# Position rows and the softmax division on ScalarE, and a planner with turns at the shared port

## The chip, the core and the metric

One core of one Trainium2 chip. The time is device microseconds of one launch. The engines are TensorE (PE: matmuls and transposes), VectorE (DVE), ScalarE (ACT), GpSimd (POOL), and SyncE (SP), which issues the DMAs here. Each engine works through its own list of instructions in order and waits on semaphores for the others.

## The reference

A decoder block over 512 tokens of width 1024, with four groups of four heads of 64:

```python
hn = rms_norm(x, norm_gain)
proj = hn @ w_in                       # 1024 x 3844, split into the groups' q, k, v and gates
o_fox  = softmax(q k^T / 8 + c_i - c_j, causal) @ v          # f: c = cumsum of log_sigmoid(forget)
o_moba = softmax(q k^T / 8 + rel_bias[bucket(i - j)], top-3 blocks and own block) @ v   # m
o_sb   = stick-breaking weights, exp(log_sigmoid(z) + suffix sums of log_sigmoid(-z)) @ v   # s
o_swa  = softmax(q k^T / 8 + rel_bias[...], window 128, with a sink) @ v                # w
y = concat(o_fox * silu(fg), o_moba * silu(mg), o_sb * silu(sg), o_swa * silu(wg))
return x + y @ w_out
```

q and k of f, m and w are RMS-normalised per head. With 512 tokens the m heads have two blocks of 256, so that they see every earlier token. All is float32.

## The kernel before

Every float32 product is made from three `float32r` matmuls: an operand is split into a hi part (rounded, `hi_copy`, on ACT) and a lo part (the rest, `lo_part`, on DVE, or on POOL), and `mm3` sums hi x hi, hi x lo and lo x hi into one PSUM bank. In names, `wh_`, `xh`, `pth_`, `yh_` are hi parts and `wl_`, `xl`, `ptl_`, `yl_` lo parts.

Weights arrive in chunks of 512 KB (`raw_`), numbered over all sets in the order sv, sqk, fvf, fqk, fg, sg, mqk, mv, mg, wg, wqkv, o. For the chunks in `POOL_LO` POOL makes the lo part in pieces of 260 columns, for the others DVE in one instruction.

The program runs the groups in the order s, f, m, w, with the projections of later groups laid between the heads' work to keep PE busy. A head has four score tiles, one for each distance or block of 128 keys, 512, 384, 256 and 128 wide for s, f and m and at most 256 for w. `softmax_head` (f, m, w): scores on PE, a fused add and minimum on DVE (`pm`, `nm`: the negated maximum), exp with row sum on ACT (`sm`), reciprocal on DVE, multiplication by it, then four rounds of transposes on PE (`pT_`), their hi and lo parts (`pth_`, `ptl_`) and the product with v (`o_f`, `o_s` and so on). `sb_head` (s): Abs, Exp, Ln on ACT (`l_`), a maximum, a scan and a difference on DVE (`pm_s`), exp on ACT, then the same transposes. The first digit of a number in these names is the head, the second the tile. `sqk` holds the scaled q and k of the s heads, `qs_` and `k00` to `k11` their hi and lo halves. `frow`, `fS` and `fxb` carry the forget sums into the f heads. `oc_`, `gate_`: a head pair's output and its gate.

`rel_rows` spreads the 32 bucket values of the relative bias over 512 distances (`relrow`, 8 rows), writes them to DRAM and spreads them from there to 128 partitions, from where `load_band` reads each head's band. `relrow` lies in the buffer that `fxb0`, and so `fS`, uses later.

The program order isn't the order in which the engines run. All instructions are collected, `_steps` finds their dependences, and `_plan` simulates the engines with a cost for each instruction: at each step the engine that can start first takes, of its instructions that can start within `PATIENCE` ns of the earliest, the one of lowest priority number. That number is the place in the program plus `TURN` of the kind of work. `MARGIN` is added to the latency of a result that another engine waits for. DVE instructions with two operands in SBUF, and all of POOL's, also wait for one modelled port. `order_engines` fixes the planned order on each engine.

Of the kernel before, what the change touches and what calls it, by code (L numbers as in the profile page):

```python
# [12 lines left out]
AF = mybir.ActivationFunctionType  # L13
ALU = mybir.AluOpType
# [24 lines left out]
REL_AT = "fg"  # L39
SQK_BANKS, R_BANK = ["sc", "tp", "tp", "pv"], "pj"  # L40

RATE, OUTU = 4.54, 0.55

POOL_LO = {1, 4, 6, 9, 10, 12, 15, 16, 17, 19, 21, 23, 24, 34, 36, 37, 38}
PIECE = 260
DVE_SQ = {(1, 1), (2, 1), (3, 0), (3, 1)}

OCUT, WARM, WARM_GAPS = 2, 3, 8


TURN = {"xn": 207, "gate": 18, "qk": -250, "v": -71, "s": 14, "pt": -313, "ot": 134, "gap":
        100000, "y": 10, "fb": 5, "w": 108, "pv": 16, "oc": 186, "nat": 0, "proj": 61, "x": -110}
PATIENCE = {"Pool": 10, "PE": 54}

MARGIN = {"PE": 100, "Activation": 41}


BOUNDS = list(range(17)) + [21, 27, 35, 46, 59, 77, 99, 128, 166, 216, 280, 363, 470]
# [18 lines left out]
def block_kernel(ctx, tc, x, xT, w_in, w_out, small, rel, out):  # L77
    nc = tc.nc
# [72 lines left out]
    if WARM:  # L151
# [3 lines left out]
        pt = pv("warm")  # L155
# [109 lines left out]
    for n in LOADS.split():  # L265
        k = int(n[1:] or 0)
# [264 lines left out]
    def softmax_head(g, h, Q, K, V, vcol, bias, nblk):  # L531
        pm = sb.tile([P, 1280], F32, tag="pm", name=f"pm_{g}{h}", bufs=2)
        off, blocks = 0, {}
        for i in range(NT):
            w = nblk(i)
            n = w * P
            blocks[i] = (off, w)
            s, s2 = scores(g, h, i, n, Q, K)
            seg = pm[:, off:off + n]
            b = bias(i, n)  # L540
            if s2 is not None:
                nc.vector.tensor_tensor(seg, s2, b, op=ALU.add)
                b = seg
            nm = cp.tile([P, 1], F32, tag="nm", name=f"nm_{g}{h}{i}", bufs=4)
            sm = cp.tile([P, 1], F32, tag="sm", name=f"sm_{g}{h}{i}", bufs=4)

            init = nsk[:, h:h + 1] if g == "w" else 3.0e38
            nc.vector.tensor_tensor_reduce(seg, s, b, scale=-1.0, scalar=init,  # L548
                                           op0=ALU.add, op1=ALU.min, accum_out=nm)
            nc.scalar.activation(seg, seg, AF.Exp, scale=-1.0, bias=nm, accum_out=sm)  # L550
            if g == "w":
                es = cp.tile([P, 1], F32, tag="es", name=f"es_{g}{h}{i}", bufs=2)
                nc.scalar.activation(es, sk[:, h:h + 1], AF.Exp, bias=nm)
                nc.vector.tensor_tensor(sm, sm, es, op=ALU.add)
            nc.vector.reciprocal(sm, sm)
            nc.vector.tensor_scalar(seg, seg, sm, None, op0=ALU.mult)
            off += n
            yield
        for res in pt_tiles(g, h, pm, blocks):
            yield  # L560
        out_half(g, h, finish_head(g, h, res, V, vcol))
        yield
# [126 lines left out]
    def rel_rows():  # L689


        re = cp.tile([8, 32], F32, tag="re", name="re")
        nc.sync.dma_start(re, rel)
        row = sb.tile([8, T], F32, tag="fxb0", name="relrow")
        neg = sb.tile([8, 127], F32, tag="fxb1", name="relneg")
        nc.gpsimd.memset(neg, NEG)
        nc.gpsimd.tensor_copy(row[:, :16], re[:, :16])
        for b, (d0, d1) in enumerate(zip(BOUNDS, BOUNDS[1:] + [T])):
            if b >= 16:
                nc.gpsimd.tensor_copy(row[:, d0:d1], re[:, b:b + 1].to_broadcast([8, d1 - d0]))  # L700
        nc.gpsimd.memset(row[:4, 128:], NEG)
        nc.sync.dma_start(rd1[:, :127], neg)
        nc.sync.dma_start(rd1[:, 127:], row)
        for h0, g in ((4, "m"), (0, "w")):
            n = wide[g]
            nc.sync.dma_start(rd[g], rd1[None, h0:h0 + 4, :n].to_broadcast([P, 4, n]))
# [204 lines left out]
class _Step:  # L911
# [20 lines left out]
    def cost(self):  # L932
        n = self.writes[0].cols if self.writes else 1
        if self.eng == "PE":
            if "const" in self.reads[0].name:
                return n * 8 / 2.4
            if "float32r" in str(self.ins.ins[0].dtype):
                return n * 0.422 + 11
            return 112 if any("ident" in a.name for a in self.reads) else n * 4 / 2.4 + 11
        if self.kind == "DMACopy":  # L940
            return 1040 if self.eng == "Pool" else 60
        if self.eng == "Activation":
            if self.kind == "LoadActFuncSet":
# [24 lines left out]
        return 50
# [67 lines left out]
def _plan(steps, moved, held_back, turn, patience, margin):  # L1036

    at = {s.ins.name: s.k for s in steps}
    after = [[] for _ in steps]
    behind = [[] for _ in steps]  # L1040
    open_ = [0] * len(steps)
    ready = [0.0] * len(steps)
    for s in steps:
        for k in s.ends:
            after[k].append(s.k)
        starts = s.starts - s.ends
        if s.ins.name in held_back:
            starts.add(at[held_back[s.ins.name]])
        for k in starts:
            behind[k].append(s.k)  # L1050
        open_[s.k] = len(s.ends) + len(starts)
    free, can, queue, rings = {}, {}, 0.0, []
    port = {"Pool": 0.0, "DVE": 0.0}
    other = {"Pool": "DVE", "DVE": "Pool"}
    for s in steps:
        free[s.eng] = 600.0
        can.setdefault(s.eng, [])
        if not open_[s.k]:
            can[s.eng].append(s.k)
    prio = [s.k + sum(turn.get(n, 0) for n in moved.get(s.ins.name, ())) for s in steps]  # L1060

    def start(e, k):
        t = max(free[e], ready[k])
        return max(t, port[other[e]]) if steps[k].port else t

    plan = []
    for _ in steps:
        t, e = min((start(e, k), e) for e in can for k in can[e])
        _, k, t = min((prio[k], k, start(e, k)) for k in can[e]
                      if start(e, k) <= t + patience.get(e, 0))  # L1070
        s = steps[k]
        can[s.eng].remove(k)
        src, end = s.eng, t + s.cost()
        plan.append((s, t, end))
        free[s.eng] = end
        if s.port:
            port[s.eng] = end
        if s.kind == "DMACopy":

            big = max(a.cols * a.parts for a in s.reads + s.writes)  # L1080
            if s.eng == "Pool":
                queue = max(t + 1680, queue) + big * 4 / 335.0
            else:
# [59 lines left out]
```

## Time and profile before

| | |
|---|---|
| runs, us | 290.61, 290.74, 292.94 (median 290.74) |
| profiled execution, us | 290.52 |
| its span, us | 288.7 |
| TensorE busy, us | 280.4 (1529 matmuls) |
| VectorE busy, us | 233.6 |
| ScalarE busy, us | 193.8 |
| GpSimd busy, us | 89.5 |
| granted TensorE clock | 1.00 |

The span runs from the first to the last instruction; the launch around it takes 1.8 us more. Busy times are sums of the instructions' durations without overlap. Matmuls overlap in the array, so that a 128x512 matmul lasts 0.40 us and one starts each 0.23 us. A row of a timeline has the start, the duration of the group, the engine, the line, output and inputs without their numbers, and in brackets the idle time ahead of it with what ended it.

### The profile page before, as it was taken

To read this page: it belongs to the slowest core of one execution; us is meant where nothing else is said; L and a number is where in the kernel's file an instruction comes from. 1 tells how busy PE (TensorE), PEld (TensorE's weight loads), DVE (VectorE), ACT (ScalarE), POOL (GpSimd) and SP (SyncE) were. 2 spreads that over 40 slices of the span, in tenths; PEclk is the share of its full clock that TensorE was granted. 3 is DMA by queue.
4 is the path that set the end of the run, shared out by engine and by line. 5 is a ranking of instruction groups with operands and counts; after the bars stand their busy time and mean duration, and the time that the engine had idled before them with its cause. 6 is when DMAs were issued, how large, how long until landed. Compare 5 with 4: busy or idle time off the path is not lost.

```text
span 288.7 us, 4641 instructions
## 1 busy us (share of the span) xinstructions
PE 280.4 (97%) x1529; PEld 235.9 (82%) x1529; DVE 233.6 (81%) x606; ACT 193.8 (67%) x445; POOL 89.5 (31%) x140
## 2 busy tenths in 40 slices
PE   8999998999999899999999999999999999999995
PEld 8998888888887678887798988788888886888884
DVE  2869289888998897669999789776989979996653
ACT  4784288957895947288895669569957877765300
POOL 5608045320029562135494000006200656001010
PEclk9999999999999999999999999999999999999999
DMA  7996342251023259621155240514001545200024
GB/s 236 333 400 191 116 151 76 70 176 44 0 74 105 95 152 287 171 73 38 41 143 148 73 145 2 183 36 145 3 18 72 173 138 168 89 2 0 2 110 182
DMA packets 19960, 33.65 MB, mean 117 GB/s; under 512 B 1616, under 2 KB 10068, under 8 KB 19808
## 3 DMA queue, kind: packets, MB, share of 16 engines
q1 hardware_dynamic: 19504, 32.96, 36.9%
q10 hardware_dynamic: 432, 0.39, 0.5%
q8 instruction: 12, 0.20, 0.3%
q14 instruction: 12, 0.10, 0.1%
HBM read 31.22 MB, written 4.22 MB: 123 GB/s over the span
## 4 chain that ended last, share of the span: by engine, by line
PE 68%; DVE 20%; ACT 8%; DMA 2%; issue 1%; ACTq 0%
PE o L342 5%; PE o L341 5%; PE o L340 4%; DVE pm_s L592 3%; PE p_wqkv L342 3%; PE p_wqkv L341 3%; PE p_wqkv L340 3%; PE p_sqk L341 2%; PE p_sqk L340 2%; PE p_sqk L342 2%; PE p_fqk L341 2%; PE p_fqk L340 2%; PE p_fqk L342 2%; DMA raw_sv<-in_w_in 2%; PE pT_m L522 2%; DVE pm_f L548 1%
## 5 line engine op out<-in xcount | busy, mean ns | idle before, releaser
L252 POOL TENSOR_TENSOR wl_fqk<-raw_fqk,wh_fqk 128x260 fp32r<-128x260 f32 (+1 forms) x12 | 11.8, 1010 | 18.9 <-ACT wh_fqk L137 18.9
L491 POOL TENSOR_TENSOR oc_f<-oc_f,gate_f 128x512 f32<-128x512 f32 x2 | 2.6, 1297 | 43.1 <-ACT gate_f L754 43.1
L676 POOL TENSOR_SCALAR fxb<-fbc,scol 128x512 f32<-128x512 f32 (+3 forms) x16 | 10.4, 654 | 17.4 <-DVE qs_f L144 10.4
L592 DVE TENSOR_TENSOR_SCAN pm_s<-l 128x512 f32<-128x512 f32 (+3 forms) x16 | 15.0, 942 | 0.1
L252 POOL TENSOR_TENSOR wl_sg<-raw_sg,wh_sg 128x256 fp32r<-128x256 f32 x8 | 7.0, 914 | 25.0 <-ACT wh_sg L137 25.0
L342 PE MATMUL p_fqk<-wh_fqk,xl 128*128 128x512 f32 x32 | 12.8, 401 | 0.0
L340 PE MATMUL p_mqk<-wh_mqk,xh 128*128 128x512 f32 x32 | 12.8, 400 | 0.0
L340 PE MATMUL p_wqkv<-wh_wqkv,xh 128*128 128x512 f32 x32 | 12.8, 399 | 0.0
L341 PE MATMUL p_mqk<-wl_mqk,xh 128*128 128x512 f32 x32 | 12.8, 399 | 0.0
L340 PE MATMUL p_fqk<-wh_fqk,xh 128*128 128x512 f32 x32 | 12.7, 403 | 0.0
L341 PE MATMUL p_fqk<-wl_fqk,xh 128*128 128x512 f32 x32 | 12.7, 397 | 0.0
L341 PE MATMUL p_wqkv<-wl_wqkv,xh 128*128 128x512 f32 x32 | 12.7, 396 | 0.0
L342 PE MATMUL p_mqk<-wh_mqk,xl 128*128 128x512 f32 x32 | 12.7, 396 | 0.0
L342 PE MATMUL p_wqkv<-wh_wqkv,xl 128*128 128x512 f32 x32 | 12.7, 396 | 0.0
L340 PE MATMUL p_sqk<-xh,wh_sqk 128*128 128x512 f32 x32 | 12.5, 389 | 0.0
L341 PE MATMUL p_sqk<-xl,wh_sqk 128*128 128x512 f32 x32 | 12.3, 390 | 0.0
L342 PE MATMUL p_sqk<-xh,wl_sqk 128*128 128x512 f32 x32 | 12.2, 392 | 0.0
L491 POOL TENSOR_TENSOR oc_w<-oc_w,gate_w 128x512 f32<-128x512 f32 x2 | 2.6, 1290 | 29.9 <-DVE oc_w L486 29.9
L142 DVE TENSOR_TENSOR ptl_s<-pT_s,pth_s 128x384 fp32r<-128x384 f32 (+3 forms) x16 | 7.4, 484 | 4.9 <-ACT pth_s L137 4.8
L142 DVE TENSOR_TENSOR ptl_m<-pT_m,pth_m 128x384 fp32r<-128x384 f32 (+3 forms) x16 | 7.3, 484 | 4.1 <-ACT pth_m L137 4.1
L137 ACT ACTIVATE pth_m<-pT_m 128x384 fp32r<-128x384 f32 (+3 forms) x16 | 6.5, 435 | 5.6 <-PE pT_m L522 5.4
L594 ACT ACTIVATE pm_s<-pm_s 128x512 f32<-128x512 f32 (+3 forms) x16 | 7.3, 465 | 4.1 <-DVE pm_s L593 3.9
(354 smaller groups left out, 1118.9 us busy)
## 6 DMA issues: line engine op xcount, KB each, us to landing
raw_o<-in_w_out SPq DMA_DIRECT2D x8, 512.0 KB, 3.2
xT<-in_xT SPq DMA_DIRECT2D x8, 256.0 KB, 4.1
raw_sqk<-in_w_in SPq DMA_DIRECT2D x4, 512.0 KB, 5.9
x<-in_x SPq DMA_DIRECT2D x8, 256.0 KB, 6.0
raw_fqk<-in_w_in SPq DMA_DIRECT2D x4, 512.0 KB, 3.7
raw_mqk<-in_w_in SPq DMA_DIRECT2D x4, 512.0 KB, 3.6
raw_wqkv<-in_w_in SPq DMA_DIRECT2D x4, 512.0 KB, 3.6
xr<-in_x SPq DMA_DIRECT2D x4, 512.0 KB, 3.8
```

The lines of the kernel that those rows point to most:

```text
L137: nc.scalar.activation(dst, src, AF.Copy if isinstance(scale, float) else AF.Identity, scale=scale)
L142: nc.vector.tensor_tensor(dst, src, hi.bitcast(F32), op=ALU.subtract)
L252: nc.gpsimd.tensor_tensor(lv[q], rv[q], hv[q].bitcast(F32), op=ALU.subtract)
L340: nc.tensor.matmul(dst, ah, bh, start=first, stop=False)
L341: nc.tensor.matmul(dst, ah, bl, start=False, stop=False)
L342: nc.tensor.matmul(dst, al, bh, start=False, stop=last)
L491: nc.gpsimd.tensor_tensor(oc, oc, gates[e], op=ALU.mult)
L522: nc.tensor.transpose(pt[:, a * P:(a + 1) * P], pm[:, o:o + P], ident)
L548: nc.vector.tensor_tensor_reduce(seg, s, b, scale=-1.0, scalar=init, op0=ALU.add, op1=ALU.min, accum_out=nm)
L592: nc.vector.tensor_tensor_scan(seg, l, l, 0.0, ALU.add, ALU.bypass)
L594: nc.scalar.activation(seg, seg, AF.Exp)
L676: nc.gpsimd.tensor_scalar(b, bc[:, i * P:], -1.0, scol[:, i, h:h + 1], op0=ALU.mult, op1=ALU.add)
```

## The change

The 15 copies of `rel_rows` move from POOL to ACT (the two MEMSETs stay on POOL). In `softmax_head` the tiles wider than 256, eight of 128x512 and eight of 128x384 in the f and m heads, are multiplied by the reciprocal on ACT in place of DVE. POOL's list loses the chunks 6, 17 and 38 (the first of fvf, the first of mqk, the last of o) to DVE and gains 30 and 32 (the last of wqkv, the second of o); 39 doesn't exist. The planner gets other turns, patience and margins, another cost for a matmul, and plans port instructions on POOL with a lead of 120 ns in its choice.

```diff
-RATE, OUTU = 4.54, 0.55
+RATE, OUTU = 4.54, 0.4
-POOL_LO = {1, 4, 6, 9, 10, 12, 15, 16, 17, 19, 21, 23, 24, 34, 36, 37, 38}
+POOL_LO = {1, 4, 9, 10, 12, 15, 16, 19, 21, 23, 24, 30, 32, 34, 36, 37, 39}
...
-TURN = {"xn": 207, "gate": 18, "qk": -250, "v": -71, "s": 14, "pt": -313, "ot": 134, "gap":
+TURN = {"xn": 215, "gate": 80, "qk": -250, "v": -68, "s": 14, "pt": -264, "ot": 322, "gap":
...
-PATIENCE = {"Pool": 10, "PE": 54}
-MARGIN = {"PE": 100, "Activation": 41}
+PATIENCE = {"Pool": 10, "PE": 21, "Activation": 29}
+MARGIN = {"PE": 100, "Activation": 52}
+LEAD = {"Pool": 120, "DVE": 0}
...
             nc.vector.reciprocal(sm, sm)
-            nc.vector.tensor_scalar(seg, seg, sm, None, op0=ALU.mult)
+            if n > 256:
+                nc.scalar.activation(seg, seg, AF.Copy, scale=sm)
+            else:
+                nc.vector.tensor_scalar(seg, seg, sm, None, op0=ALU.mult)
...
-        nc.gpsimd.tensor_copy(row[:, :16], re[:, :16])
+        nc.scalar.activation(row[:, :16], re[:, :16], AF.Copy)
         for b, (d0, d1) in enumerate(zip(BOUNDS, BOUNDS[1:] + [T])):
             if b >= 16:
-                nc.gpsimd.tensor_copy(row[:, d0:d1], re[:, b:b + 1].to_broadcast([8, d1 - d0]))
+                nc.scalar.activation(row[:, d0:d1], re[:, b:b + 1].to_broadcast([8, d1 - d0]),
+                                     AF.Copy)
...
-                return n * 0.422 + 11
+                return max(n * 0.4167 + 15, 109)
...
     def start(e, k):
+
         t = max(free[e], ready[k])
-        return max(t, port[other[e]]) if steps[k].port else t
+        if not steps[k].port:
+            return t, t
+        t += LEAD[e]
+        return max(t, port[other[e]]), t
...
-        t, e = min((start(e, k), e) for e in can for k in can[e])
-        _, k, t = min((prio[k], k, start(e, k)) for k in can[e]
-                      if start(e, k) <= t + patience.get(e, 0))
+        (t, _), e = min((start(e, k), e) for e in can for k in can[e])
+        _, k, t = min((prio[k], k, start(e, k)[0]) for k in can[e]
+                      if start(e, k)[0] <= t + patience.get(e, 0))
         s = steps[k]
+        t -= LEAD[e] if s.port else 0
```

The plan comes out otherwise at many places. Three of them follow, without the rows' numbers. The last number in a name counts tiles and differs by a few between the two programs.

DVE at the start of the s heads, where it makes the lo halves of q (`qs_s10`, `qs_s11`) and k (`k00`); before:

```order
L144 SCALAR_TENSOR_TENSOR qs_s10_480<-sqk1_478,qs_s10_480 64x512
L144 SCALAR_TENSOR_TENSOR qs_s11_483<-sqk1_478,qs_s11_483 64x512
L142 TENSOR_TENSOR k00_138<-sqk2_511,k00_138 64x512
L142 TENSOR_TENSOR k01_140<-sqk2_511,k01_140 64x512
L786 TENSOR_TENSOR sqk3_574<-p_sqk3_519,rrow_135 128x512
L739 TENSOR_SCALAR fsp_151<-p_fvf0_582,rx_129 128x4
```

and of the change:

```order
L792 TENSOR_TENSOR sqk3_572<-p_sqk3_517,rrow_135 128x512
L745 TENSOR_SCALAR fsp_151<-p_fvf0_580,rx_129 128x4
L146 SCALAR_TENSOR_TENSOR qs_s10_478<-sqk1_476,qs_s10_478 64x512
L146 SCALAR_TENSOR_TENSOR qs_s11_481<-sqk1_476,qs_s11_481 64x512
L144 TENSOR_TENSOR k00_138<-sqk2_509,k00_138 64x512
L144 TENSOR_TENSOR k01_140<-sqk2_509,k01_140 64x512
```

`sqk3` and the small `fsp` step now stand ahead of three lo halves. On PE the matmuls that need the lo half of `k00` stood behind four matmuls of `p_fvf1` and now stand behind nineteen of them.

ACT at the last head of the s group (`l_30`, `l_31` are its first two tiles, `pm_s2` belongs to the head before); before:

```order
L589 ACTIVATE l_31_1258<-l_31_1258 128x384
L590 ACTIVATE l_30_1246<-l_30_1246,one_89 128x512
L590 ACTIVATE l_31_1258<-l_31_1258,one_89 128x384
L594 ACTIVATE pm_s2_1024<-pm_s2_1024 128x128
L137 ACTIVATE wh_mqk2_1312<-raw_mqk2_1110 128x1024
L137 ACTIVATE pth_s23_1152<-pT_s23_1147 128x512
L594 ACTIVATE pm_s3_1242<-pm_s3_1242 128x512
```

and of the change, where eight copies of `relrow` already stand ahead of these rows:

```order
L599 ACTIVATE pm_s2_1022<-pm_s2_1022 128x128
L705 ACTIVATE relrow_1174<-re_1172 8x29
L705 ACTIVATE relrow_1174<-re_1172 8x38
L705 ACTIVATE relrow_1174<-re_1172 8x50
L705 ACTIVATE relrow_1174<-re_1172 8x64
L705 ACTIVATE relrow_1174<-re_1172 8x83
L705 ACTIVATE relrow_1174<-re_1172 8x107
L139 ACTIVATE pth_s23_1147<-pT_s23_1142 128x512
L705 ACTIVATE relrow_1174<-re_1172 8x42
L594 ACTIVATE l_31_1253<-l_31_1253 128x384
L139 ACTIVATE wh_mqk2_1307<-raw_mqk2_1108 128x1024
L595 ACTIVATE l_31_1253<-l_31_1253,one_89 128x384
```

The copies, `pm_s2` and `pth_s23` moved ahead of the Exp of `l_31`, and `wh_mqk2` ahead of its Ln. On PE the first use of `wl_mqk2` moved ahead by the work of 25 matmuls of 128x512. On DVE the MEMSET of `fS` moved ahead of `gate_s0`.

ACT in the first two f heads (L550 and L552 are the exp with its row sum, L559 is the new multiplication); before:

```order
L550 ACTIVATE pm_f0_1496,sm_f00_1501<-pm_f0_1496,nm_f00_1500 128x512
L550 ACTIVATE pm_f0_1496,sm_f01_1552<-pm_f0_1496,nm_f01_1551 128x384
L137 ACTIVATE k11_144<-kT_f1_1457,small_69 64x512
L550 ACTIVATE pm_f0_1496,sm_f02_1561<-pm_f0_1496,nm_f02_1560 128x256
L550 ACTIVATE pm_f0_1496,sm_f03_1570<-pm_f0_1496,nm_f03_1569 128x128
```

and of the change:

```order
L552 ACTIVATE pm_f0_1491,sm_f00_1496<-pm_f0_1491,nm_f00_1495 128x512
L139 ACTIVATE k10_142<-kT_f1_1452,small_69 64x512
L139 ACTIVATE k11_144<-kT_f1_1452,small_69 64x512
L559 ACTIVATE pm_f0_1491<-pm_f0_1491,sm_f00_1496 128x512
L552 ACTIVATE pm_f0_1491,sm_f01_1547<-pm_f0_1491,nm_f01_1546 128x384
L139 ACTIVATE k11_144<-kT_f1_1452,small_69 64x512
L552 ACTIVATE pm_f0_1491,sm_f02_1556<-pm_f0_1491,nm_f02_1555 128x256
L559 ACTIVATE pm_f0_1491<-pm_f0_1491,sm_f01_1547 128x384
```

Between an exp and the multiplication of its tile the plan puts one or two other instructions, hi copies of k or the next exp.

In the w heads' beginning, DVE makes `yl_m1`, the lo part of the m heads' second output, ahead of the third fused step of `pm_w0` and of the addition to `sm_w00`; before, both came first. One piece of `wo6` stands ahead of `oc_m1` on POOL.

More of the change, by code (lines that the diff above doesn't have):

```diff
@@ L48 @@
 OCUT, WARM, WARM_GAPS = 2, 3, 8
-TURN = {"xn": 207, "gate": 18, "qk": -250, "v": -71, "s": 14, "pt": -313, "ot": 134, "gap":
-        100000, "y": 10, "fb": 5, "w": 108, "pv": 16, "oc": 186, "nat": 0, "proj": 61, "x": -110}
-PATIENCE = {"Pool": 10, "PE": 54}
-MARGIN = {"PE": 100, "Activation": 41}
+TURN = {"xn": 215, "gate": 80, "qk": -250, "v": -68, "s": 14, "pt": -264, "ot": 322, "gap":
+        100000, "y": 7, "fb": 5, "w": 81, "pv": -29, "oc": 258, "nat": -5, "proj": 65, "x": -110}
+PATIENCE = {"Pool": 10, "PE": 21, "Activation": 29}
+MARGIN = {"PE": 100, "Activation": 52}
+LEAD = {"Pool": 120, "DVE": 0}
 BOUNDS = list(range(17)) + [21, 27, 35, 46, 59, 77, 99, 128, 166, 216, 280, 363, 470]
```

## The prediction

> **What bounds the kernel now.** I read the page's busy shares first, then the waits of TensorE, then the busy time stretch by stretch.
>
> ```profile
> span 288.7 us, 4641 instructions
> ...
> PE 280.4 (97%) x1529; PEld 235.9 (82%) x1529; DVE 233.6 (81%) x606; ACT 193.8 (67%) x445; POOL 89.5 (31%) x140
> ```
>
> TensorE (PE) is busy for 280.4 of 288.7 us. The change leaves its matmuls as they are and only reorders them, so no term of my sum can be larger than the time in which PE waits. The profiled execution took 290.52 us, 1.8 us more than its span; the median of the runs shown is 290.74, so both bases agree within 0.1%.
>
> ```profile
> PE pT_s L522 <- ACT pm_s L594: 0.9, 2, 0.6
> ...
> PE s_s L510 <- DVE k L142: 0.7, 1, 0.7
> PE o L342 <- DVE yl_m L142: 0.6, 1, 0.6
> PE s_s L509 <- DVE pm_s L593: 0.5, 1, 0.5
> PE s_s L509 <- ACT k L137: 0.4, 1, 0.4
> ```
>
> These are PE's waits with total, times and longest (those of the start are left out). They sum to 3.1 us. So it is a kernel whose every gain must come out of a handful of short stalls. Where do they stand, and who is full there? In the next view the columns are PE, PEld, DVE, ACT and POOL busy in each stretch.
>
> ```profile
> 40.00:60.00 20.00, 18.35 (x128) 16.44 (x127) 18.44 (x31) 17.77 (x32) 11.57 (x12) 1.00 0.31 97
> ...
> 80.00:100.00 20.00, 19.19 (x92) 15.22 (x90) 18.16 (x34) 15.99 (x36) 13.01 (x29) 1.00 0.29 83
> 100.00:120.00 20.00, 19.71 (x100) 16.08 (x101) 14.89 (x31) 10.94 (x25) 7.23 (x8) 1.00 0.81 224
> 120.00:140.00 20.00, 19.80 (x101) 15.16 (x100) 17.27 (x46) 15.49 (x34) 8.83 (x21) 1.00 0.21 65
> 140.00:160.00 20.00, 19.76 (x136) 17.91 (x135) 19.94 (x67) 15.37 (x41) 11.37 (x20) 1.00 0.38 106
> ...
> 240.00:260.00 20.00, 19.37 (x105) 15.52 (x105) 19.74 (x78) 13.57 (x46) 3.07 (x5) 1.00 0.31 93
> ```
>
> PE's lost time lies at 40–60 us (1.65, the start of the stick-breaking heads), 80–120 (1.1, their end), 120–160 (0.44, the f heads) and 240–260 (0.63). In three of these places VectorE (DVE) is near full: 18.44, 19.94, 19.74 of 20 us. ScalarE (ACT) has room: 15.4 of 20 in the f heads, 10.94 at 100–120. The granted clock is 1.00 throughout, so no term is owed to it.
>
> **Part 1: the reordered start, 40–60 us.** PE's timeline shows the stall and, behind it, the pace of the 128x260 matmuls, one each 0.12 us:
>
> ```profile
> 45.34 0.68 PE L510 MATMUL s_s<-k,qs_s 128*128 128x512 f32 x2 [0.71 <-DVE k L142]
> 45.85 0.28 PE L341 MATMUL p_fvf<-wl_fvf,xh 128*128 128x260 f32 x1
> 45.97 0.28 PE L342 MATMUL p_fvf<-wh_fvf,xl 128*128 128x260 f32 x1
> ```
>
> DVE's timeline before it:
>
> ```profile
> 40.47 0.68 DVE L144 SCALAR_TENSOR_TENSOR qs_s<-sqk,qs_s 64x512 fp32r<-64x512 f32 x1
> 41.18 3.39 DVE L144 SCALAR_TENSOR_TENSOR qs_s<-sqk,qs_s 64x512 fp32r<-64x512 f32 x3
> 44.60 1.40 DVE L142 TENSOR_TENSOR k<-sqk,k 64x512 fp32r<-64x512 f32 x2
> 46.03 0.69 DVE L786 TENSOR_TENSOR sqk<-p_sqk,rrow 128x512 f32<-128x512 f32 x1
> ```
>
> GpSimd (POOL) in the same time:
>
> ```profile
> 39.82 4.21 POOL L252 TENSOR_TENSOR wl_fqk<-raw_fqk,wh_fqk 128x260 fp32r<-128x260 f32 x4 [10.79 <-ACT wh_fqk L137]
> ```
>
> And ACT's wait behind it:
>
> ```profile
> 46.76 1.29 ACT L137 ACTIVATE k<-sqk 64x512 fp32r<-64x512 f32 x2 [0.84 <-DVE sqk L786]
> ```
>
> The second matmul of the first scores waits 0.71 us for the lo half of `k00`. DVE was late there because three `qs_s` steps took 3.39 us, 1.13 each, while POOL made `wl_fqk`; the one before them had got through beside POOL in 0.68, and the two `k` steps after POOL's end took 0.70 each. In the new order DVE makes `sqk3` (0.69) and one small step (some 0.2) ahead of the last two, so `k00` comes about 0.9 us later. But PE puts fifteen 128x260 matmuls ahead of the second halves, 15 x 0.12 = 1.8 us of work. The 0.71 is overpaid by 1.8 - 0.9 = 0.9 us, so it goes: **-0.7**. ACT no longer waits 0.84 for `sqk3`, so the exps behind it come about as much earlier, and the 0.7 is not simply taken back at the next wait (s_s for pm_s, 0.5), which I leave at its size. If instead ACT's 0.84 is not won, the next wait takes all of it: this term lies between -0.7 and 0.
>
> **Part 2: the rows of relative positions, 94–107 us.** What POOL paid for the copies, and the nearest operation of ACT:
>
> ```profile
> L700 POOL COPY relrow<-re 8x5 f32<-8x5 f32 (+13 forms) x14 | 2.2, 203 | 0.0
> ```
>
> ```profile
> L284 ACT ACTIVATE r0f<-rmf 128x8 f32<-128x8 f32 x4 | 0.7, 200 | 2.7 <-DVE rmf L283 2.7
> ```
>
> ACT's timeline where they now go, and DVE's gate behind that place:
>
> ```profile
> 98.05 1.23 ACT L590 ACTIVATE l<-l,one 128x512 f32<-128x512 f32 x2
> ...
> 104.16 0.63 ACT L594 ACTIVATE pm_s<-pm_s 128x512 f32<-128x512 f32 x1 [2.64 <-DVE pm_s L593]
> ```
>
> ```profile
> 106.78 0.69 DVE L748 TENSOR_TENSOR gate_s<-p_sg,rrow 128x512 f32<-128x512 f32 x1 [0.39 <-PE p_sg L342]
> ```
>
> Off POOL: 14 copies in 2.2 us and one more of the kind. That earns nothing by itself, since POOL is no bound. On ACT the nearest row has 200 ns: 15 x 0.2 = 3.0 us at most, and 1.5 if neighbours overlap by half; I take 2.5, near the row. They stand between the Ln of `l_30` and the Exp of `l_31`. Before, both Ln were done at 98.05 + 1.23 = 99.3, and ACT stood idle 2.64 us ahead of 104.16, so the 2.5 fit into that gap. With them and a 1.0 us `wh_mqk2`, which now also goes first, the Ln of `l_31` ends near 99.3 + 3.5 = 102.8. DVE needs it for a step of 0.5 us and then a scan, after which the exp of `pm_s3` at 106.8 and PE's `pT_s3` come; DVE was busy with the step ahead of it until 104.1 (it releases ACT's row at 104.16), so the cover is about 104.1 - 103.3 = 0.8 us.
>
> The two waits for `pm_s` should go: `mqk0` leaves POOL here, so DVE's steps beside it shorten, and PE has 1.3 us more work ahead of the third `pT_s2` pair and 0.5 ahead of the fourth, against 0.6 and 0.3: **-0.9**. But PE then comes 0.7 + 0.9 = 1.6 us earlier, against a cover of 0.8. A new wait at the chain l_31, pm_s3, exp, `pT_s3` takes about **+0.8** back; its bounds are 0 (the whole chain is earlier too) and 2.5 (no cover, and all copies on the path).
>
> Two queues stand behind that.
>
> ```profile
> 101.12 4.39 POOL L252 TENSOR_TENSOR wl_mqk<-raw_mqk,wh_mqk 128x260 fp32r<-128x260 f32 x4 [2.30 <-ACT wh_mqk L137]
> ```
>
> ```profile
> 115.96 0.40 PE L341 MATMUL p_mqk<-wl_mqk,xh 128*128 128x512 f32 x1
> ```
>
> `wl_mqk2` is made from about 102.8 on in place of 101.12; 4.4 us later is 107.2. PE asked for it at 115.96; its new order asks 5.8 us of work earlier (25 matmuls of 128x512 at 0.23, 0.12 scaled by columns), and the gains 1.6 more: 108.6. So 1.4 us are left and I cost it at nothing; beyond that each us is a us of PE. The MEMSET of `fS` shares its buffer with `relrow` and now stands ahead of `gate_s0` on DVE; were `relrow` still on its way to DRAM then, the gate and `oc_s` would queue behind it. The copies end by about 102 and the gate ran at 106.78: I count nothing.
>
> **Part 3: dividing on ACT, f and m heads.** DVE's groups for the f heads, which the change removes, and ACT's nearest operation, also with a scale per row:
>
> ```profile
> L556 DVE TENSOR_SCALAR pm_f<-pm_f,sm_f 128x384 f32<-128x384 f32 x4 | 2.2, 550 | 0.0
> ...
> L556 DVE TENSOR_SCALAR pm_f<-pm_f,sm_f 128x512 f32<-128x512 f32 x4 | 1.9, 472 | 0.0
> ```
>
> ```profile
> L137 ACT ACTIVATE xh<-xT,small 128x512 fp32r<-128x512 f32 x8 | 5.5, 716 | 0.1
> ```
>
> DVE loses 1.9 + 2.2 = 4.1 us in the f heads, and I take the same for the m heads, which have the same tiles. ACT gains 4 x 0.72, and 4 x 0.6 for 128x384 (the row scaled by columns would be 0.54; I take some fixed part): 5.3 us in each. The work grows by 1.2 us a group but moves from the engine with 19.94 of 20 to one with 15.4. PE's idle in 120–160 is only 0.44 us, so this buys **-0.2**; its bounds are -0.44 and the loss of the third rival below.
>
> The Trainium skill, "ScalarE: Activation LUTs", section "Rules for kernel authors", says that `mul` belongs on VectorE, not ScalarE. Per operation the rows agree (716 against 472 ns). By that rule alone the 1.2 us a group would be lost in both groups, 2.4 in place of 0.2 won, and the sum 291.4; by the rows of 120–160 DVE is the full engine, the loss is hidden, and I keep 288.8.
>
> **Part 4: the m heads' output, 240–244 us.** DVE's timeline ahead of PE's wait for `yl_m`:
>
> ```profile
> 239.50 0.62 DVE L554 TENSOR_TENSOR sm_w<-sm_w,es_w 128x1 f32<-128x1 f32 x1
> 240.05 1.31 DVE L142 TENSOR_TENSOR yl_m<-oc_m,yh_m 128x512 fp32r<-128x512 f32 x1
> ```
>
> PE's 0.6 for `yl_m` goes if DVE reaches it earlier. In the new order the third pair of `pm_w0` steps (about 0.5) and the 0.62 add come behind it: 1.1 us earlier, against 0.6: **-0.6**, but for a GpSimd piece of `wo6` that now stands ahead of `oc_m1`.
>
> **Sum:** -0.7 - 0.9 + 0.8 - 0.2 - 0.6 = -1.6, and from the profiled 290.52 that is 288.9; I say **288.8 us**, a tenth lower, for waits of under 0.1 us that the view does not list.
>
> **Rivals.** *All of it comes through.* If the l_31 chain is not late, and the waits of pm_s and k also fall to the earlier ACT, PE's 3.1 us and the 0.44 of the f heads go: 290.5 - 3.5 = 287.0. For it: DVE was near full at every stall. Against it: each stall removed brings PE sooner to the next chain.
>
> *The waits only change names.* Each chain of s, exp and pT still goes through two engines in order; if PE's lead is lost in the f heads, where DVE was full, the end is 290.5.
>
> *ACT becomes the bound of the f heads: slower.* There the new multiply waits in ACT's queue for DVE's reciprocal, with the next exps and `pth_f` behind it, and PE's `o_f` behind those. At 120–160 ACT is busy 15.49 + 15.37 = 30.9 of 40 us; with 5.3 it is 36.2. It decides from (40 - 36.2) / 8 = 0.48 us of waiting per multiply, which is one DVE step of that stage ahead of the reciprocal. With two steps, 0.95: 36.2 + 7.6 - 40 = 3.8 us lost, less the 1.6 won elsewhere: 292.7. Against it: the order puts other work between exp and multiply at most tiles. (The ScalarE rule named above points to this rival.)
>
> **How the numbers follow.** Forecast 0.57, all 0.15, names only 0.14, slower 0.14. The range reaches from just below 287.0 to just below 292.7: 286.6 to 292.4. About 1%, 2.9 us, is what a measurement of this kernel tells from no change. Faster by more (below 287.8): the second case and a fifth of the first, 0.26. Slower by more (above 293.6): half of the last, 0.07. Within: 0.67.
>
> **What would show it.** The wait of `s_s` for `k` near 45 us and that of `o` for `yl_m` near 240 gone; ACT about 2.5 us of copies near 99–101; a new short wait of PE at 102–112 for `pm_s` or `ptl_s`; DVE near 225 us busy and ACT near 207; PE's matmul time unchanged. I am wrong if ACT in the f heads shows long waits for `sm_f`, if PE waits for `wl_mqk`, or if a stall appears in the m or w heads, where I assume none.

## The result and the profile after

| | before | changed |
|---|---|---|
| median of 13 runs each, us | 290.74 (290.03 to 292.94) | 288.70 (288.08 to 289.43) |
| profiled execution, us | 290.52 | 288.08 |
| its span, us | 288.7 | 286.3 |

The ratio is 0.9933 with a 95% interval of 0.9918 to 0.9949: a gain of 0.7%, 2.0 us, which is small but clear of no change.

The busy shares of the changed kernel, and the waits of TensorE in total, times and longest:

```profile
span 286.3 us, 4633 instructions
...
PE 280.3 (98%) x1529; PEld 235.3 (82%) x1529; DVE 223.4 (78%) x591; ACT 203.1 (71%) x476; POOL 82.1 (29%) x122
```

```profile
PE warm L160 <- PEq L1146: 0.8, 1, 0.8
PE s_s L511 <- ACT k L139: 0.4, 1, 0.4
PE s_s L507 <- DVE fS L662: 0.3, 1, 0.3
PE pT_m L524 <- ACT k L139: 0.2, 1, 0.2
PE pT_m L524 <- DVE qs_m L146: 0.2, 1, 0.2
PE qT_m L455 <- DVE qs_m L146: 0.2, 1, 0.2
```

PE's work is the same (280.3 against 280.4 us), so all of the gain is waiting that went. The first row belongs to the start, as it did before. Of the waits shown of before only the 0.4 for ACT's `k` is left. `pT_s`, `k` on DVE, `yl_m` and `pm_s` are gone. New are 0.3 at an `s_s` and three short waits in the m heads (`pT_m`, `qT_m`). The same stretches as before, with PE, PEld, DVE, ACT and POOL busy, and one more, 160–180:

```profile
40.00:60.00 20.00, 19.50 (x131) 17.37 (x131) 17.28 (x34) 18.43 (x35) 10.02 (x11) 1.00 0.30 86
...
80.00:100.00 20.00, 19.89 (x98) 16.20 (x97) 19.39 (x37) 16.73 (x48) 8.38 (x10) 1.00 0.45 133
100.00:120.00 20.00, 19.71 (x104) 15.78 (x103) 14.51 (x32) 11.01 (x28) 5.12 (x7) 1.00 0.60 159
120.00:140.00 20.00, 19.85 (x101) 15.33 (x101) 17.34 (x52) 17.98 (x41) 11.21 (x27) 1.00 0.32 93
140.00:160.00 20.00, 20.00 (x147) 18.41 (x147) 18.28 (x59) 17.41 (x43) 9.32 (x16) 1.00 0.42 119
160.00:180.00 20.00, 19.46 (x110) 15.66 (x110) 15.88 (x34) 17.45 (x33) 0.00 (x0) 1.00 0.25 67
...
240.00:260.00 20.00, 19.96 (x116) 16.70 (x115) 19.71 (x85) 13.48 (x53) 1.30 (x1) 1.00 0.20 69
```

PE lost 1.65 us at 40–60 before and loses 0.50 now; at 80–120 it lost 1.10 and loses 0.40, at 120–160 0.44 and 0.15, at 240–260 0.63 and 0.04. At 160–180, where it lost nothing, it loses 0.54. The row of before for that stretch:

```profile
160.00:180.00 20.00, 20.00 (x125) 17.60 (x124) 16.71 (x37) 14.53 (x26) 0.00 (x0) 1.00 0.27 79
```

A stretch of the clock holds other work in each program, and a short wait hides in busy time, since a matmul that lasts 0.40 us is still running when the next one, due 0.23 us after it, is late. For sums I use a measure worked out from PE's timeline. Each matmul's start, less the PE work ahead of it at PE's own pace (0.229 us per 128x512, 0.176 per 384, 0.118 per 256 or 260 columns, 0.109 per transpose, 0.058 per other matmul of 128 columns; by this pace all of PE's work is 268.0 us), is PE's lateness; what it grows by is waiting. In us, by stretches of PE *work*, not of the clock (30–50 is the start of the s heads, 80–120 their end, 120–160 the f heads, 160–210 the m heads, 210–250 the end of these and the start of the w heads; rows e1 to e12 are the experiments below):

```
run    to 10 10-30 30-50 50-80 80-120 120-160 160-210 210-250 250-268
before  5.50 -0.06  2.55  0.65   2.21    2.91    0.78    2.66    0.08
after   4.81 -0.02  1.11  0.55   1.83    2.44    2.11    1.95    0.06
e1      5.37 -0.08  1.15  0.43   1.89    5.10    1.73    4.26    0.06
e2      5.51  1.12  2.54  0.63   1.06    2.91    1.65    5.31    0.04
e3      5.53 -0.02  1.11  0.58   2.27    2.44    2.12    1.91    0.07
e4      5.19 -0.07  1.11  0.52   1.86    5.37    1.39    4.06    0.06
e5      6.23 -0.02  1.13  0.49   1.25    3.94    1.95    1.60    0.05
e6      5.64  0.07  2.54  0.58   2.13    5.16    2.64    3.52    0.11
e7      4.97  1.22  1.59  0.59   2.32    3.57    0.81    2.16    0.08
e8      5.05  0.17  1.13  0.49   1.82    2.45    1.93    1.63    0.07
e9      5.38 -0.07  1.13  0.55   1.72    2.46    1.38    1.61    0.08
e10     4.94 -0.07  1.59  0.63   2.26    3.59    0.78    2.13    0.10
e11     5.34 -0.07  1.11  0.49   1.25    2.43    1.38    3.29    0.33
e12     5.60 -0.07  0.08  2.59   2.30    2.47    1.38    1.61    0.05
```

Before to after: -1.44 at 30–50, -0.38 at 80–120, -0.47 in the f heads, **+1.33 in the m heads**, -0.71 at 210–250. The first column is not the change's: in the changed kernel and e3, e5, e8 and e9, which run that part in one order, it lies between 4.81 and 6.23, as the first weights arrive sooner or later. The 1.1 and 1.2 of e2 and e7 at 10–30 are a late arrival too, of rows of `x`: DVE waits 1.39 and 1.68 us for them, and `wh_sqk` on ACT, for which PE waits, comes behind. So 0.7 of the 2.4 us between the two profiled executions is chance, and the 1.7 us behind it stand beside 2.0 between the medians.

### The profile page after: what moved, and what is told of

Same layout as the page of the kernel before. It is cut to its first block, busy times and chain, and to the rows that moved or that the text cites. A ratio compares the mean times of both kernels' runs of the same rounds, so it can differ in the third digit from the quotient of the medians.

```text
span 286.3 us, 4633 instructions
## 1 busy us (share of the span) xinstructions
PE 280.3 (98%) x1529; PEld 235.3 (82%) x1529; DVE 223.4 (78%) x591; ACT 203.1 (71%) x476; POOL 82.1 (29%) x122
## 4 chain that ended last, share of the span: by engine, by line
PE 63%; DVE 15%; ACT 15%; POOL 2%; DMA 2%; issue 2%; DVEq 0%
PE o L343 4%; PE o L344 4%; PE o L342 4%; ACT k L139 3%; PE p_fqk L342 2%; PE p_fqk L344 2%; PE p_sqk L343 2%; PE p_sqk L342 2%; PE p_wqkv L343 2%; PE p_fqk L343 2%; PE p_wqkv L342 2%; PE p_wqkv L344 2%; PE p_sqk L344 2%; POOL wl_o L254 2%; PE p_mqk L344 2%; PE p_mqk L343 2%
## 5 line engine op out<-in xcount | busy, mean ns | idle before, releaser
L254 POOL TENSOR_TENSOR wl_fqk<-raw_fqk,wh_fqk 128x260 fp32r<-128x260 f32 (+1 forms) x12 | 10.9, 932 | 23.0 <-ACT wh_fqk L139 23.0
L254 POOL TENSOR_TENSOR wl_sg<-raw_sg,wh_sg 128x256 fp32r<-128x256 f32 x8 | 7.8, 1009 | 24.3 <-ACT wh_sg L139 24.3
L597 DVE TENSOR_TENSOR_SCAN pm_s<-l 128x512 f32<-128x512 f32 (+3 forms) x16 | 13.7, 858 | 0.1
L681 POOL TENSOR_SCALAR fxb<-fbc,scol 128x512 f32<-128x512 f32 (+3 forms) x16 | 9.6, 604 | 10.6 <-DVE nm_f L550 6.1
L254 POOL TENSOR_TENSOR wl_o<-raw_o,wh_o 128x260 fp32r<-128x260 f32 (+1 forms) x8 | 6.7, 864 | 17.9 <-ACT wh_o L139 17.6
L552 ACT ACTIVATE pm_m<-pm_m,nm_m 128x512 f32<-128x512 f32 (+3 forms) x16 | 8.8, 553 | 2.3 <-DVE nm_m L550 2.3
L552 ACT ACTIVATE pm_w<-pm_w,nm_w 128x256 f32<-128x256 f32 (+1 forms) x16 | 7.6, 477 | 3.6 <-DVE nm_w L550 3.5
```

Source lines behind the costliest of these rows:

```text
L254: nc.gpsimd.tensor_tensor(lv[q], rv[q], hv[q].bitcast(F32), op=ALU.subtract)
L597: nc.vector.tensor_tensor_scan(seg, l, l, 0.0, ALU.add, ALU.bypass)
L681: nc.gpsimd.tensor_scalar(b, bc[:, i * P:], -1.0, scol[:, i, h:h + 1], op0=ALU.mult, op1=ALU.add)
```

## Experiments

In the expectations, theories A, B, C and D are named anew with each question. All ratios are to the kernel before, run beside the kernel on the same chip.

**e1 and e2: the change's two halves.** e1 takes the planner's numbers and POOL's chunks alone; copies stay on POOL and divisions on DVE.

```diff
-POOL_LO = {1, 4, 6, 9, 10, 12, 15, 16, 17, 19, 21, 23, 24, 34, 36, 37, 38}
+POOL_LO = {1, 4, 9, 10, 12, 15, 16, 19, 21, 23, 24, 30, 32, 34, 36, 37, 39}
...
-PATIENCE = {"Pool": 10, "PE": 54}
+PATIENCE = {"Pool": 10, "PE": 21, "Activation": 29}
...
```

> The changed kernel's planner numbers and chunk list, with the 15 copies back on GpSimd and all divisions back on VectorE. Theory A (the order makes the gain): the stalls at 45, 94-100 and 241 us go as in the changed kernel, and its new waits of 160-190 us (about 1.3 us in its trace) go too: 287.5 to 288.7 us. Theory B (the moved operations make the gain, by relieving VectorE and the shared port): 290 to 291 us.

e2 takes the moved operations alone, under the old numbers.

```diff
-            nc.vector.tensor_scalar(seg, seg, sm, None, op0=ALU.mult)
+            if n > 256:
+                nc.scalar.activation(seg, seg, AF.Copy, scale=sm)
+            else:
+                nc.vector.tensor_scalar(seg, seg, sm, None, op0=ALU.mult)
...
-        nc.gpsimd.tensor_copy(row[:, :16], re[:, :16])
+        nc.scalar.activation(row[:, :16], re[:, :16], AF.Copy)
...
```

> The kernel before, its planner numbers and chunk list kept, with only the copies and the wide divisions moved to ScalarE. Theory A: VectorE still makes k00 ahead of sqk3 and yl_m behind the w heads' steps, so the stalls at 45 and 241 us stay, and ScalarE's new work adds waits in the m heads: 290 to 292 us. Theory B: 288.5 to 289.5 us.

Measured: e1 1.0083 (1.0059 to 1.0107), e2 1.0061 (1.0038 to 1.0084); medians 293.68 and 292.76 us. Every range missed, that of e2's theory A by 0.8 us: each half alone is **slower** than before, and together they are faster. e1 already has the new start of the s heads (1.15 at 30–50) and loses 5.10 in the f heads and 4.26 at 210–250; e2 keeps the old start (2.54) and loses 5.31 at 210–250. PE's waits of e1, and then of e2:

```profile
PE pT_f L524 <- DVE ptl_f L144: 1.1, 1, 1.1
PE o L342 <- DVE v_w L146: 0.9, 1, 0.9
...
PE o L342 <- DVE part L854: 0.8, 1, 0.8
```

```profile
PE s_w L509 <- DVE nm_w L548: 1.3, 2, 1.1
...
PE o L340 <- ACT yh_m L137: 0.7, 1, 0.7
```

**e3 and e4: one moved operation put back, all else as changed, planned afresh.** e3: the copies on POOL.

```diff
-        nc.scalar.activation(row[:, :16], re[:, :16], AF.Copy)
+        nc.gpsimd.tensor_copy(row[:, :16], re[:, :16])
...
```

> The changed kernel with the 15 copies back on GpSimd and nothing else undone. Theory A: the copies on ScalarE cost the new wait of 0.3 to 0.45 us at 103.8 us, so 288.2 to 288.7 us, no slower than the changed kernel. Theory B (taking the copies off GpSimd frees the port): 289 us or more.

e4: the divisions on DVE.

```diff
-            if n > 256:
-                nc.scalar.activation(seg, seg, AF.Copy, scale=sm)
-            else:
-                nc.vector.tensor_scalar(seg, seg, sm, None, op0=ALU.mult)
+            nc.vector.tensor_scalar(seg, seg, sm, None, op0=ALU.mult)
```

> The changed kernel with all divisions back on VectorE. Theory A: the waits of the m heads behind ScalarE's queue (1.3 us at 160-190 us) go, the f heads lose the 0.4 us that they won at 120-160: 287.7 to 288.5 us. Theory B: VectorE is full again at 140-160 us and the f heads' gain goes with more waits behind it: 289.5 us or more.

Measured: e3 0.9933 (0.9910 to 0.9956), the changed kernel's own ratio, as theory A has it, though its median of 289.19 us (before: 291.03 on that chip) would by itself fall to B. So with a fresh plan the copies' engine is worth nothing that can be measured here. Between e1 and e4, which differ in the copies alone and have the divisions on DVE, it is 0.32%, at the edge of what the intervals separate. e4 1.0051 (1.0031 to 1.0072), in theory B's range: without the division on ACT the gain turns into a loss, again in the f heads (5.37) and at 210–250 (4.06). That reads as if the division were worth 1.2%. But the plan was made afresh for e4, and so its order changed too.

**e5 and e6: order and division apart.** Both plan the 16 wide divisions as if they stood on the one engine, and issue them on the other at their planned place; every other row keeps its order. e5: the changed kernel's order, divisions on DVE (the same operations on the same engines as e4).

```diff
+        self.real = self.eng
...
+            self.eng = "Activation"
+            self.kind = 'Activation'
...
+    for s, t, _ in plan:
+        lists.setdefault(s.real, []).append((t, s))
+    for e in {s.real for s, _, _ in plan if s.eng != s.real}:
+        lists[e].sort(key=lambda p: p[0])
```

> The changed kernel's order on every engine kept row for row; only the 16 wide divisions run on VectorE again, put into its row where the plan had them on ScalarE. Theory C (the planner's numbers only fit the program that they were tuned for, and a plan made afresh puts things badly): 288.7 to 290 us, about as the changed kernel. Theory D (VectorE is the bound of the f and m heads, so the division's place itself is worth the time): 291.5 to 293 us, with PE waiting on VectorE at 126-150 and 215-230 us.

e6: the order of before, divisions on ACT, by the same means.

```diff
+            self.eng = "DVE"
+            self.kind = 'TensorScalarPtr'
```

> The kernel before, its order on every engine kept row for row; only the 16 wide divisions run on ScalarE, in its row where the plan had them on VectorE. Theory C: 290 to 291.5 us, no gain to speak of, PE's stalls at 45, 94-100 and 241 us stay. Theory D: VectorE relieved of 8 us where it is full, 288.5 to 290 us. ScalarE's queue as bound (the slower rival of the prediction): 291.5 us or more.

Measured: e5 0.9959 (0.9942 to 0.9977), e6 1.0167 (1.0144 to 1.0190). e4 and e5 differ in nothing but the order, and lie 0.9% (2.7 us) apart. So the new numbers are not a better planner for every program: of the plans made afresh by them, those with the f heads' divisions on ACT gain (the changed kernel, e3, and e11 below), and those without lose (e1, e4). The new order, with the copies and the chunk list that belong to it, is worth 0.41%. The division's move adds 0.26% in it (a difference of two ratios, good to about 0.24). The same move in the old order costs 1.67%. PE's waits and the stretch 140–160 of e6:

```profile
PE pT_m L522 <- ACT pm_m L557: 2.3, 3, 1.0
PE o_f L472 <- ACT pth_f L137: 1.7, 3, 0.8
```

```profile
140.00:160.00 20.00, 18.26 (x120) 16.13 (x119) 16.72 (x58) 17.86 (x45) 10.96 (x20) 1.00 0.38 105
```

ACT's timeline of e6, and the matmul that waits for its last row:

```profile
141.18 1.05 ACT L137 ACTIVATE wh_mv<-raw_mv 128x1024 fp32r<-128x1024 f32 x1
142.13 1.22 ACT L557 ACTIVATE pm_f<-pm_f,sm_f 128x512 f32<-128x512 f32 x2
143.24 0.53 ACT L137 ACTIVATE pth_f<-pT_f 128x256 fp32r<-128x256 f32 x2
```

```profile
143.66 0.39 PE L472 MATMUL o_f<-pth_f,v_f 128*128 128x256 f32 x1 [0.84 <-ACT pth_f L137]
```

This is the prediction's slower rival, with one correction: ACT doesn't stand idle for the reciprocal (no division of e6 shows a wait for `sm_f`). The divisions run back to back with what is queued, here 1.22 us ahead of `pth_f`, and what stands behind them is late. The larger waits, for `pm_m` (2.3) and `pm_f` (0.7), are for divisions that themselves stand behind other work. Here one that ACT starts at 185.32, behind 1.04 us of `wh_wqkv`:

```profile
185.97 0.33 PE L522 MATMUL pT_m<-ident,pm_m 128*128 128x128 f32 x1 [1.02 <-ACT pm_m L557]
```

ACT is not full at 17.86 of 20. In the changed kernel it has 17.41 in this stretch, and PE loses nothing there, so it is the order of ACT's queue that decides, and not its load.

In the new order the same move helps where the prediction put it. The stretch 140–160 of e5, and one of its PE waits:

```profile
140.00:160.00 20.00, 19.13 (x135) 17.18 (x134) 19.66 (x63) 15.74 (x39) 9.91 (x16) 1.00 0.40 119
```

```profile
PE pT_f L524 <- DVE pm_f L558: 0.8, 1, 0.8
```

DVE 19.66 against 18.28 in the changed kernel; f heads 3.94 against 2.44.

**e7 and e10: two and three of the prediction's moves in the old order by hand.** e7 puts `sqk3` and `fsp` ahead on DVE, `k00`'s second matmuls later on PE and `wh_fqk1` later on ACT (part 1), and `yl_m1` earlier (part 4).

```diff
+    if e == "DVE":
+        q = at(l, "qs_s10")
+        shift(l, at(l, "sqk3"), q)
+        shift(l, at(l, "fsp"), q + 1)
+        shift(l, at(l, "yl_m1"), at(l, "nm_w02"))
+    if e == "PE":
+        for n in range(2):
+            a = at(l, f"s_s0{n}", 1)
+            shift(l, a, a + 16)
+    if e == "Activation":
+        shift(l, at(l, "wh_fqk1"), at(l, "v_f0") + 1)
```

> The kernel before with two local moves of the changed one and nothing else: at 45 us sqk3 and fsp go ahead of qs_s10 on VectorE, the second halves of the first scores 15 matmuls later on PE, wh_fqk1 behind v_f0 on ScalarE; at 241 us yl_m1 goes ahead of the third step of pm_w0. Theory A (each stall goes by itself and its time is kept): 0.7 to 1.0 us less lateness of PE behind 50 us, 0.6 us less behind 245: 289.2 to 289.8 us. Rival (time won early is taken back by the next chain): 290.3 to 291 us.

e10 adds `pT_s2`'s later transposes on PE (part 2).

```diff
+        for t in ("pT_s22", "pT_s23"):
+            a = at(l, t, 3) if t == "pT_s23" else None
+            if a is not None:
+                shift(l, a, a + 3)
+            a = at(l, t, 2)
+            shift(l, a, a + 7)
```

> The kernel with two local moves (start of the s heads, yl_m1), and as a third the last transposes of pT_s2 later on PE: the third pair by six matmuls of p_fg1, the fourth pT_s23 by two of p_sg0. Copies, mqk0 and everything else of GpSimd stay. If PE's order alone removes the waits for pm_s (1.0 us in the run with two moves): PE's lateness between 80 and 100 us falls from 2.1 to about 1.2, time 288.9 to 289.4 us. If mqk0's leaving GpSimd was needed: the waits stay above 0.5 us, 289.6 us or more.

Measured: e7 0.9974 (0.9958 to 0.9990; 289.88 us, just above what A gave and below its rival), e10 0.9949 (0.9931 to 0.9966). e7's PE waits, with neither the `k` of DVE nor `yl_m` in the list:

```profile
PE pT_s L522 <- ACT pm_s L594: 1.0, 2, 0.6
...
PE o_f L473 <- DVE ptl_f L142: 0.7, 1, 0.7
PE s_w L509 <- DVE nm_w L548: 0.6, 1, 0.6
PE p_sqk L340 <- ACT wh_sqk L137: 0.5, 1, 0.5
```

Both stalls go: -0.96 at 30–50 and -0.50 at 210–250. But 0.66 comes back in the f heads, at `o_f`: PE, which no longer has the stall, now waits for the next late thing. So part 1 and part 4 are real, and part of what they win is returned downstream unless the engines behind it move as well. Of e10's third move PE's growth shows 0.06 (2.32 to 2.26 at 80–120): the waits for `pm_s` fall from 1.0 to 0.3 there, and others come, so that neither of the two cases of its expectation came true. The two intervals overlap, and PE's order alone doesn't bring the 0.9 that part 2 gave it; whether it brings a little stays open.

**e8 and e11: dividing on ACT in the f heads alone.** e8 keeps the changed order, by the means of e5, and e11 plans afresh.

```diff
-            if n > 256:
+            if n > 256 and g == "f":
```

> The changed kernel's order on every engine kept; only the eight wide divisions of the m heads run on VectorE again. If ScalarE's queue makes the new waits of the m heads (pT_m and qT_m at 169-178 us, about 0.9 us in the changed kernel's trace): 287.8 to 288.4 us. By theory D VectorE comes late there: 289.5 us or more.

> The same operations on the same engines as the run with the changed kernel's order and the m divisions on VectorE (287.9 us), but with the plan made afresh by the same planner numbers. Theory C (the numbers fit one program): slower, 289 to 292.5 us. If the assignment of the divisions is what counts: 287.5 to 288.3 us.

Measured: e8 **0.9913** (0.9892 to 0.9934), e11 0.9943 (0.9920 to 0.9967). e8's time (287.86 us) came out as expected, but not for the reason given: the m heads still lose 1.93 (2.11 in the changed kernel), and 0.32 less at 210–250 counts for more. e8 is 0.2% below the changed kernel, which these intervals don't separate. e5 and e8 ran side by side and differ only in the f heads' eight divisions: 289.42 and 287.86 us, 1.56 apart, and the f heads lose 3.94 and 2.45. So in the new order these eight are worth about 0.5%, the clearest gain that any of the moved operations shows; the eight of the m heads win nothing that can be measured. Between e8 and e11 only the order differs: in the two profiles the fresh plan wins 0.55 in the m heads and 0.57 at 80–120 and loses 1.66 at 210–250 (1.63 and 3.29). The two ratios lie 0.30% apart, which their intervals just fail to separate.

**e9: e8 with two more edits.** `l_31`'s Exp and Ln go ahead of the copies on ACT, and `m0` and `m2` divide their 128x512 tile on ACT.

```diff
+        for n, f in enumerate(("Exp", "Ln")):
+            l.insert(q + n, l.pop(at("l_31", f)))
...
+            if n > 256 and (g == "f" or g == "m" and n == 512 and h in (0, 2)):
```

> The changed kernel's order with three edits: the Exp and Ln of l_31 ahead of the relrow copies on ScalarE; in the m heads the divisions of heads 1 and 3 and the 128x384 tiles of heads 0 and 2 on VectorE, the 128x512 tiles of heads 0 and 2 on ScalarE. If the chain l_31, scan, pm_s3 is what PE waits for at 104 us, that wait (0.3 by the view, 0.45 by PE's pace) shrinks by 0.2 to 0.4; the waits for pT_m at 175 and 208 us of the run with all m divisions on VectorE (0.6 and 0.5) go: 286.8 to 287.6 us. Rival (won time is taken back by the next chain): 287.8 to 288.7 us.

Measured: **0.9906** (0.9887 to 0.9925), 288.14 us beside 290.88, in the range of its rival, but with e8 the fastest kernel of the study. The m heads lose 0.55 less than in e8 (1.38 against 1.93). The `l_31` edit won 0.1: the wait at 104 us went, and another stands ahead of it, at 98.3:

```profile
PE pT_s L524 <- ACT pm_s L599: 0.5, 1, 0.5
```

**e12: e9 with `k` first.** The last long wait of the s heads' start is `s_s` for ACT's `k00`. e12 puts `k00` and `k01` ahead of `qs_s10` on ACT and of `sqk3` on DVE, and `k10` and `k11` later on both.

```diff
+        for k in ("k00", "k01"):
+            for n in range(2):
+                shift(at(k, n), at("qs_s10"))
+        for k in ("k10", "k10", "k11", "k11"):
+            shift(at(k), at("l_03", 1))
```

> The run with mixed divisions and one more edit at the start of the s heads: the hi and lo halves of k00 and k01 go ahead of those of qs_s10 and qs_s11, and those of k10 and k11 (wanted some 25 us later) go behind the first head's work, on ScalarE and VectorE. If PE's wait for k00 at 43 us (0.4 by the view, 0.6 by PE's pace, the same in all runs so far) is only a matter of that order, and ScalarE freed of 2.5 us keeps the next chain early: 0.6 to 0.8 us less, 287.0 to 287.6 us. Rival (the next chain, l_00 to pm_s0, takes it back): 287.9 to 288.3 us.

Measured: 0.9935 (0.9912 to 0.9958), 288.97 us, above both ranges. The stall went completely (0.08 at 30–50, from 1.13), and 2.04 came back at 50–80. ACT's timeline and PE's waits:

```profile
56.93 2.55 ACT L139 ACTIVATE k<-sqk 64x512 fp32r<-64x512 f32 x4
59.51 0.31 ACT L593 ACTIVATE l<-l 128x128 f32<-128x128 f32 x1
```

```profile
PE pT_s L524 <- ACT pm_s L599: 1.3, 2, 0.7
PE o_s L474 <- ACT pth_s L139: 1.2, 1, 1.2
```

The edit put four `k` rows of 2.55 us to where they weren't yet needed, and there they stand ahead of the last tile (`l_03`) of the first s head.

## Why the prediction was right, and where it was not

288.8 was predicted and 288.70 measured. The sum of its steps was -1.6 us; the waits behind the start fell by 1.7. The total agrees better than its terms.

**Part 1 (-0.7, measured -1.44).** PE passes the place of the stall without waiting; the rows of PE at 45 us have no bracket any more:

```profile
45.49 0.28 PE L342 MATMUL p_fvf<-wh_fvf,xh 128*128 128x260 f32 x1
45.61 0.57 PE L512 MATMUL s_s<-k,qs_s 128*128 128x512 f32 x2
```

By e7 the local move is worth 0.96, more than the 0.71 in the view. The rest is the next wait, "s_s for pm_s, 0.5", which the prediction left at its size: 0.66 at PE's pace before, 0.22 after.

**Part 2 (-0.9 + 0.8, measured -0.38).** Both waits for `pm_s` went. Which of the prediction's two causes did it is open: e10 tried the later transposes on PE without `mqk0`'s leaving POOL, and they brought little. The chain through `l_31` did become late, by the path that was worked out:

```profile
98.63 0.51 ACT L594 ACTIVATE l<-l 128x384 f32<-128x384 f32 x1
99.04 1.04 ACT L139 ACTIVATE wh_mqk<-raw_mqk 128x1024 fp32r<-128x1024 f32 x1
99.99 0.60 ACT L595 ACTIVATE l<-l,one 128x384 f32<-128x384 f32 x1
```

```profile
100.62 0.56 DVE L596 SCALAR_TENSOR_TENSOR l<-s_s,l 128x384 f32<-128x384 f32 x1 [0.71 <-ACT l L595]
...
101.63 1.50 DVE L597 TENSOR_TENSOR_SCAN pm_s<-l 128x384 f32<-128x384 f32 x1
...
103.22 0.54 DVE L598 TENSOR_TENSOR pm_s<-s_s,pm_s 128x384 f32<-128x384 f32 x1
...
103.71 0.06 DVE L662 MEMSET fS<- 4x1 f32 x1
```

```profile
103.82 0.39 PE L507 MATMUL s_s<-k,qs_s 128*128 128x256 f32 x1 [0.29 <-DVE fS L662]
```

But PE's wait is at the next score matmul and not at `pT_s3`, and it is 0.29, not 0.8. The label `fS` is a coincidence: the matmul needs the PSUM bank (one of two for scores) that the row at 103.22 leaves free at 103.76, the moment in which the MEMSET ends as well. In e3 the same matmul waits for `pm_s` by name. The size was wrong because the copies came earlier (96.1–98.7, not 99–101) and the cover was larger. In e3, with the copies on POOL, this chain reaches its scan 0.87 us earlier, so ACT's copies seem to make it late; but there the scan takes 2.23 us in place of 1.50, and PE waits 0.65:

```profile
100.76 2.23 DVE L597 TENSOR_TENSOR_SCAN pm_s<-l 128x384 f32<-128x384 f32 x1
```

With POOL idle a scan of this size took 0.95 in all three traces (before, changed, e3). POOL makes `wl_mqk` beside both of these scans; but beside the same work the scan of before took 0.94, so why these two are long is open.

**Part 3, f heads (-0.2, measured -0.47).** The direction is shown by e5, which has 1.50 more there with the divisions on DVE; e6 shows that the rival's mechanism is real in another order. The multiply costs what the `xh` row had given:

```profile
L559 ACT ACTIVATE pm_f<-pm_f,sm_f 128x512 f32<-128x512 f32 x4 | 2.9, 724 | 1.0 <-DVE sm_f L557 1.0
...
L559 ACT ACTIVATE pm_f<-pm_f,sm_f 128x384 f32<-128x384 f32 x4 | 2.5, 618 | 0.1
```

The Trainium skill, "ScalarE: Activation LUTs", section "Rules for kernel authors", sends `mul` to VectorE. Per operation that holds (724 ns here, 472 on DVE). For the kernel the two orders answer differently: the move brings 0.26% in the new order, against the rule, and costs 1.67% in the old one, in agreement with it.

**Part 3, m heads: the step that failed.** The prediction took the m heads as free of stalls (0); they lose 1.33. ACT's timeline and one of the new waits:

```profile
173.43 0.72 ACT L559 ACTIVATE pm_m<-pm_m,sm_m 128x512 f32<-128x512 f32 x1
174.18 1.38 ACT L139 ACTIVATE k<-kT_m,small 64x512 fp32r<-64x512 f32 x2
...
176.81 0.68 ACT L139 ACTIVATE k<-kT_m,small 64x512 fp32r<-64x512 f32 x1
177.51 0.62 ACT L559 ACTIVATE pm_m<-pm_m,sm_m 128x384 f32<-128x384 f32 x1
```

```profile
177.54 0.33 PE L524 MATMUL pT_m<-ident,pm_m 128*128 128x128 f32 x1 [0.22 <-ACT k L139]
```

ACT works through `k` halves and divisions without a gap, and the transposes stand right behind them. It is tempting to blame the divisions, but e5 and e8 make them on DVE in the same order and lose as much (1.95 and 1.93 against 2.11). So most of it is the order; e9's mixture wins 0.55 of it back. What in the order makes PE wait was isolated by no run. The trace and the kernel suggest a reading: `qT_m`, `kT_m` and `pT_m` take turns in two PSUM banks (`NTP`), so the first transposes of `pm_m` can't start until the halves that read `qT_m` and `kT_m` are made. PE starts at 177.54 when ACT's `k` ends at 177.49, and at 174.50 behind DVE's `qs_m`, which ends at 174.36. In e8 the same matmul waits 0.58 for `qs_m`, which there stands behind the division on DVE.

**Part 4 (-0.6, measured -0.71)** went as worked out; e7's move alone gives -0.50.

**The sum.** Too small by 0.7 in part 1, by 0.3 in part 2, 0.3 in the f heads and 0.1 in part 4, 1.4 together, against 1.3 missed in the m heads: errors that cancelled, so that the time's nearness to 288.8 is luck. Of the marks named in advance, DVE came to 223.4 (225 expected) and ACT to 203.1 (207 expected), and no wait for `wl_mqk` appeared. The mark "a stall in the m heads" did.

**The rivals.** "All of it comes through" would have needed the m heads free and the 0.4 for `k` gone. "The waits only change names" holds for e10's third move and, at the least, for e12, not for the whole. The slower rival happened in e6, at 295.42 against its 292.7: it had counted the f heads alone and only waiting time, while in e6 the m heads lose 1.86 as well. That the changed kernel escapes it is the order's doing.

## What to carry to other kernels

Where a planner's numbers were tuned, they and the program belong together: after any edit, compare the edit in the *held* order with the edit under a fresh plan, or the planner's luck is booked as the edit's worth (e4 and e5 lie 0.9% apart with the same operations on the same engines). An engine with room by its share can still be the wrong place for an operation, since what counts is what stands ahead of it and behind it in the queue. When a stall is taken away by hand, look next at the chain that PE now reaches sooner, and put nothing that isn't needed yet ahead of a chain's last tile.

## What the runs showed of the hardware that I had not expected

The start varies by chance by 1.4 us, against a gain of 2.0: with one order, PE has lost between 4.81 and 6.23 us after its first 10 us of work. The wait is for the first weights; of the changed kernel, and then of e5:

```profile
ACT wh_sv L139 <- DMA raw_sv<-in_w_in: 0.9, 2, 0.7
```

```profile
ACT wh_sv L139 <- DMA raw_sv<-in_w_in: 2.5, 3, 1.6
```

In e8, e9 and e3 this wait is 1.1, 1.5 and 1.6 us and the loss 5.05, 5.38 and 5.53, so the loss follows the wait. A single profiled execution therefore can't tell 0.5% of this kernel; repeated runs or a sum that leaves the start out can. Later stretches don't grow by this: e5, latest at the start, loses less than the other four at 80–120 (1.25). Whether that is because a late PE meets work that is done was not tested; e11 loses the same 1.25 there after a start of 5.34.
